# A two-block float32 model on one core: the depthwise convolution's accumulators and the engines of the norm behind it

## The chip, the cores and the metric

The kernel runs on one core of one Trainium2 chip. The metric is the device time of one execution in microseconds, lower is better. The core's engines run side by side: TensorE (PE; PEld is its weight load), VectorE (DVE), ScalarE (ACT), GpSimd (POOL) and SyncE (SP, which issues most transfers). SBUF is the working memory; PSUM, eight banks of 128x512 float32, holds matmul results and can be read and written by VectorE and ScalarE as well.

## The reference

A sequence of 512 tokens of width 1024 goes through two blocks. The first has two layers. Layer A mixes with a convolution, layer B with a sparse attention; the second block has an attention branch, a gated scan and a routed expert layer. Only layer A's mixer matters here:

```python
def conformer_conv(u, conv_w, conv_b, g, b):
    a, gl = jnp.split(u, 2, axis=-1)
    h = a * jax.nn.sigmoid(gl)
    h = jnp.pad(h, ((0, 0), (CONV_KERNEL - 1, 0), (0, 0)))
    h = lax.conv_general_dilated(h, conv_w[:, None, :], (1,), 'VALID',
                                 feature_group_count=CONV_WIDTH, ...) + conv_b
    return jax.nn.silu(layer_norm(h, g, b))
```

It is a depthwise convolution of 1536 channels with 31 taps along the sequence, followed by a layer norm over the channels and a SiLU. In the layer, `u`, a memory query and a gate come from one projection of `x`; the mixer's output and a cross-attention over a small memory are concatenated, multiplied by `silu(gate)`, projected by `a_w_out`, and go through a residual layer norm.

## The kernel before, in words

Activations are transposed: channels in the partitions, the 512 tokens along the free dimension. So the 1536 convolution channels are 12 tiles, `h0` to `h11`, each 128x542 with 30 zeros ahead. A float32 product is made of three matmuls (`mm3`, L164 to L166): operand and weight are each split in a high part (`hi`, a cast on ScalarE, L158 or L184) and the low rest (`lo`, a subtraction on VectorE or GpSimd, L159 or L187). `Weights` loads, splits and keeps weights in pieces of 128x1024 when they are first used; its attribute `lo` says which engine subtracts.

`layer_a` (L537) issues the work in this order. L545: twelve pairs of projections, and out of each pair `h_j` on VectorE (L552). Then the memory's keys and values (`mem_kv`, tiles `mk`, `ak`, `mvT`, `av`), four memory attentions (`mem_attn`, with the maximum `mmx` on VectorE and the exponential `mp` on ScalarE), and sixteen gates (L568), whose products L576 and L579 and the low halves of `y12` to `y15` are GpSimd's; gate tiles go to a DRAM buffer `a_gates`. Between the gates lie the keys and values of layer B (`bk`, `bv`).

The convolution (L585 to L604) has a first column, `h2`, that ScalarE multiplies and GpSimd adds. The other eleven are VectorE's: for each group of columns in the table `CGR` (L49) it runs over the 31 taps, and in a tap over the group's columns. One tap is one instruction, L602: the column shifted by `t` times a weight per partition, plus the accumulator. The first two columns of a group accumulate in a PSUM bank of the list `cv` (banks 6 and 7); a third one accumulates in the SBUF tile of tag `cva` (L594). `CGR` has one group of three, (7, 8, 9), so the third column is `h9`.

`st.add` squares each finished column on ScalarE and adds it up on GpSimd. `st.finish` sums over the channels with small matmuls (tile `cst`, L290), and spreads the mean and the reciprocal deviation over the partitions into PSUM (`Mb`, `Rb`). Then VectorE subtracts `Mb` from the twelve tiles (L607). L609 copies `Rb` to SBUF as `Rs`, since GpSimd works on SBUF. In the loop of L610 each tile is multiplied by the deviation (L614 on VectorE for every third tile, L616 on GpSimd for the others), scaled (L618), goes through the SiLU (L620 and L621) and the gate that was read back (L623), and is split for the next product; the low half is VectorE's for even tiles and GpSimd's for odd ones.

`out_proj` (L470) multiplies by `a_w_out`: for four output tiles the first eight of the 16 input tiles (`y12` to `y15`, `y0` to `y3`), then the other eight, then the remaining four output tiles in two halves of the tokens.

The program is written in a framework that keeps dependences by semaphores and chooses the order of each engine's instructions itself; each engine then works through its own list in that order, and waits where an operand isn't there. So an edit of a few lines can move the instructions of the whole layer.

Of the kernel before, what the change touches and what calls it, by code (L numbers as in the profile page):

```python
# [17 lines left out]
OP = mybir.AluOpType  # L18
# [27 lines left out]
NLO = 3  # L46
JMEM = 4
MLO = 6
CGR = (0, 1), (3, 4), (5, 6), (7, 8, 9), (10, 11)  # L49
NWARM = 8  # L50
WCUT = {0: 2, 2: 8}
WONE = 5
# [6 lines left out]
class Body:  # L59
# [249 lines left out]
    def run(self):  # L309
        nc = self.nc  # L310
# [8 lines left out]
        self.right = ExitStack()  # L319
        self.bk = self.right_pool("bk")  # L320
        if True:
            with self.phase("A", cva=1, slot=12, pcv=4, scr=2, asc=2, app=2, sq=2, accq=1, accs=1, back=4):
                with self.tc.tile_pool(name="mem", bufs=1) as self.mem:
                    self.layer_a()
            if self.stop == "a":
                self.right.close()
                return
            self.banks(mm=(0, 1), s=(2, 5), pt=(3, 4), o=(6, 7))
            with self.phase("B", slot=14, scr=4, asc=2, app=2, logit=3, alibi=2):
                self.layer_b()  # L330
# [206 lines left out]
    def layer_a(self):  # L537
        nc = self.nc
# [21 lines left out]
        Y = {}  # L560
        for h in range(4):
            f = self.scr("qm", tag="back")
            nc.scalar.copy(f, self.proj(W, 24 + h, self.X))
            o = self.mem_attn(self.split(f, f"qm{h}", lo="g"), kv, h)
            f = self.scr("mo")
# [19 lines left out]
        for j in (2,):  # L585
            for t in range(CK):
# [4 lines left out]
                    nc.gpsimd.tensor_tensor(p if t < CK - 1 else cs[j], acc, p, op=OP.add)  # L591
                acc = p
        for js in CGR:
            accs = [self.scr("cacc", tag="cva") if u == 2 else self.bank("cv", "cacc") for u in range(len(js))]  # L594
            for t in range(CK):
                for j, a in zip(js, accs):
                    wc = self.vec("conv_w", j * CK + t)
                    src = hs[j][:, t:t + T]
                    if t == 0:
                        nc.vector.tensor_scalar(a, src, wc, self.vec("conv_b", j), op0=OP.mult, op1=OP.add)  # L600
                    else:
                        nc.vector.scalar_tensor_tensor(a if t < CK - 1 else cs[j], src, wc, a, op0=OP.mult, op1=OP.add)  # L602
            for j in (2, *js) if 5 in js else js:
                st.add(cs[j])  # L604
        Rb, Mb = st.finish(CONVW, 1e-5)
        for c in cs:
            nc.vector.tensor_tensor(c, c, Mb, op=OP.subtract)  # L607
        Rs = self.scr("Rs", tag="accs")
        nc.scalar.copy(Rs, Rb)  # L609
        for j in range(12):  # L610
            c = cs[j]
            n = self.scr("cn", tag=("asc", "app")[j % 2])
            if j % 3 == 0:
                nc.vector.tensor_tensor(n, c, Rb, op=OP.mult)  # L614
            else:
                nc.gpsimd.tensor_tensor(n, c, Rs, op=OP.mult)  # L616
            c = n
            nc.scalar.activation(c, c, AF.Identity, bias=self.vec("a_ln_b", j), scale=self.vec("a_ln_g", j))  # L618
            th = self.scr("th")
            nc.scalar.activation(th, c, AF.Tanh, scale=0.5)  # L620
            nc.vector.scalar_tensor_tensor(c, th, 1.0, c, op0=OP.add, op1=OP.mult)  # L621
            y = self.back("gb", gd[j])
            nc.vector.scalar_tensor_tensor(y, c, 0.25, y, op0=OP.mult, op1=OP.mult)  # L623
            Y[4 + j] = self.split(y, f"y{j}", hi="s", lo="vg"[j % 2], x=2 <= j < 10, tag="slot" if j < 2 else "pcv")
        self.new_x()
        self.banks(alias=dict(Rb="cv", Mb="cv"), mm=(0, 1, 2, 5), pt=(3, 4), cv=(6, 7))

# [862 lines left out]
```

## Time and profile before

| | us |
|---|---|
| median of 3 runs | 2709.32 |
| lowest, highest | 2707.19, 2710.68 |
| the profiled execution | 2716.38 |
| its span, first to last instruction | 2714.4 |
| busy in it: PE, DVE, ACT, POOL | 2621.4, 2077.2, 1247.2, 952.8 |

The profile is of one execution. Busy time counts an engine's instructions from start to end, overlaps once; instructions of one engine overlap by some 0.08 us, so the distance between the starts of two of them is a little less than their duration. Matmuls are pipelined, so a busy TensorE need not be one at its peak. [...] An idle time is put down to the instruction whose completion ended it.

### The profile page before, as it was taken

The numbers are of one execution on the slowest core, as the hardware profiler recorded it, in microseconds if no ns is written. First come the engines' busy times: TensorE is split into PE (matmuls) and PEld (weight loads), VectorE is DVE, ScalarE is ACT, GpSimd is POOL, SyncE is SP. The second block draws the span as 40 slices with busy tenths as digits, with TensorE's granted clock in tenths as the row PEclk, the third lists the DMA queues.
The fourth block names the chain that finished last, engine by engine and source line by source line (L and its number), as shares of the span: only waits on it lengthen the run. The fifth ranks groups of instructions, "written<-read, shape, count | busy, mean of one in ns | idle before, by whom it ended". The sixth has DMA issues, their size and how long they took to land.

```text
span 2714.4 us, 40123 instructions
## 1 busy us (share of the span) xinstructions
PE 2621.4 (97%) x14581; PEld 2284.0 (84%) x14581; DVE 2077.2 (77%) x3926; ACT 1247.2 (46%) x2173; POOL 952.8 (35%) x654
## 2 busy tenths in 40 slices
PE   9989989999999999999999999999999999999998
PEld 7777879788889977788899999898898888888876
DVE  8999876695557678763679999888877877787765
ACT  4535554455545444333443555555543443343333
POOL 5965654332206555553431123223311121111201
PEclk9999999999999999999999999999999999999999
DMA  5233355223246311225733788788899899999952
GB/s 183 86 109 116 125 163 172 87 82 98 82 152 209 109 55 55 66 87 167 217 96 115 239 291 309 289 324 294 316 369 340 304 330 332 335 327 338 338 191 93
DMA packets 211958, 542.20 MB, mean 200 GB/s; under 512 B 18224, under 2 KB 105904, under 8 KB 192304
## 3 DMA queue, kind: packets, MB, share of 16 engines
q1 hardware_dynamic: 183488, 395.30, 44.3%
q0 software_dynamic: 18432, 134.23, 13.3%
q10 hardware_dynamic: 9840, 10.12, 1.2%
q8 instruction: 114, 1.87, 0.3%
q14 instruction: 84, 0.69, 0.1%
HBM read 468.99 MB, written 70.58 MB: 199 GB/s over the span
## 4 chain that ended last, share of the span: by engine, by line
PE 50%; DMA 14%; DVE 12%; issue 4%; ACT 2%; POOL 1%; SPq 0%; DVEq 0%; POOLq 0%; ACTq 0%
DMA grow<-peer_uv,pidx 9%; PE mm L164 9%; PE mm L165 9%; PE mm L166 8%; PE po L166 4%; PE po L164 4%; PE po L165 4%; DMA as<-a_spill 3%; PE out L164 2%; PE out L165 2%; PE out L166 2%; DVE pacc L1199 1%; DVE wlo L159 1%; DVE og L1312 1%; DVE hK L917 1%
## 5 line engine op out<-in xcount | busy, mean ns | idle before, releaser
L1189 POOL DMA_INDIRECT grow<-peer_uv,pidx x128 | 236.8, 1850 | 914.8 <-DVE pacc L1199 751.8
L158 ACT CAST whi<-wraw 128x1024 fp32r<-128x1024 f32 x360 | 377.6, 1050 | 383.9 <-PE mm L165 194.4
L159 POOL TENSOR_TENSOR wlo<-wraw,whi 128x1024 fp32r<-128x1024 f32 x157 | 380.7, 2427 | 419.6 <-ACT whi L158 360.9
L164 PE MATMUL po<-vhi,wh 128*128 128x512 f32 x768 | 297.1, 392 | 4.0 <-ACT wh L1351 4.0
L165 PE MATMUL po<-vlo,wh 128*128 128x512 f32 x768 | 299.0, 391 | 0.0
L159 DVE TENSOR_TENSOR wlo<-wraw,whi 128x1024 fp32r<-128x1024 f32 x203 | 260.1, 1283 | 48.2 <-ACT whi L158 45.4
L166 PE MATMUL po<-vhi,wl 128*128 128x512 f32 x768 | 273.6, 393 | 3.2 <-DVE wl L1352 3.2
L602 DVE SCALAR_TENSOR_TENSOR cacc<-h,vecs,cacc 128x512 f32<-128x512 f32 x319 | 240.0, 815 | 0.4
L1192 DVE SCALAR_TENSOR_TENSOR grow<-grow,hrow 128x1024 f32<-128x1024 f32 x128 | 156.6, 1223 | 101.2 <-DMA grow<-peer_uv,pidx 101.2
L166 PEld LDWEIGHTS po<-vhi,wl 128*128 128x128 f32 x768 | 143.9, 188 | 36.7 <-DVE wl L1352 6.6
L164 PEld LDWEIGHTS po<-vhi,wh 128*128 128x128 f32 x768 | 144.0, 188 | 34.2 <-ACT wh L1351 4.6
L165 PEld LDWEIGHTS po<-vlo,wh 128*128 128x128 f32 x768 | 144.3, 188 | 27.9
L159 DVE TENSOR_TENSOR vlo<-vraw,vhi 128x1024 fp32r<-128x1024 f32 x128 | 156.4, 1222 | 11.7 <-ACT vhi L158 11.6
L1199 DVE SCALAR_TENSOR_TENSOR pacc<-grow,pwc,pacc 128x1024 f32<-128x1024 f32 x127 | 162.8, 1282 | 2.3 <-ACT pwc L1195 1.8
L1194 ACT ACTIVATE pwc<-pac 128x1 f32<-128x1 f32 x128 | 25.9, 202 | 275.7 <-DVE grow L1192 275.6
L158 ACT CAST vhi<-vraw 128x1024 fp32r<-128x1024 f32 x128 | 133.8, 1046 | 34.4 <-DMA vraw<-peer_uv 18.1
L1351 ACT CAST wh<-as 128x384 fp32r<-128x384 f32 x103 | 52.6, 510 | 145.8 <-PE po L165 133.3
L1321 ACT COPY stage<-gp 128x512 f32<-128x512 f32 x96 | 96.9, 1101 | 44.9 <-PE gp L1319 44.9
L164 PE MATMUL mm<-X0h,whi 128*128 128x512 f32 (+2 forms) x294 | 109.8, 378 | 6.0 <-ACT pa L1181 2.6
L1319 PE MATMUL gp<-og,oh 128*128 128x128 bf16 x1152 | 95.7, 227 | 17.4 <-DVE og L1312 17.0
L165 PE MATMUL mm<-X2l,whi 128*128 128x512 f32 (+2 forms) x294 | 106.6, 363 | 0.6 <-DVE X2l L529 0.6
L164 PE MATMUL mm<-X2h,whi 128*128 128x512 f32 (+2 forms) x294 | 105.6, 359 | 1.4 <-ACT X2h L528 1.4
(984 smaller groups left out, 7762.8 us busy)
## 6 DMA issues: line engine op xcount, KB each, us to landing
wraw<-peer_uT SPq DMA_DIRECT2D x128, 512.0 KB, 5.7
vraw<-peer_uv SPq DMA_DIRECT2D x128, 512.0 KB, 7.0
gates<-stage SPq DMA_DIRECT2D x24, 1024.0 KB, 6.7
G<-gates SPq DMA_DIRECT2D x16, 1536.0 KB, 14.5
wraw<-a_w_in SPq DMA_DIRECT2D x43, 512.0 KB, 3.5
wraw<-c_w_in SPq DMA_DIRECT2D x42, 512.0 KB, 3.5
wraw<-b_w_in SPq DMA_DIRECT2D x39, 512.0 KB, 3.6
a_spill<-pa SPq DMA_DIRECT2D x103, 192.0 KB, 5.5
```

What stands on the lines that cost most here:

```text
L158: nc.scalar.copy(h, src)
L159: (nc.gpsimd if lo == "g" else nc.vector).tensor_tensor(l, src, h, op=OP.subtract)
L164: nc.tensor.matmul(ps, w[0], x[0], start=start, stop=False)
L165: nc.tensor.matmul(ps, w[0], x[1], start=False, stop=False)
L166: nc.tensor.matmul(ps, w[1], x[0], start=False, stop=stop)
L602: nc.vector.scalar_tensor_tensor(a if t < CK - 1 else cs[j], src, wc, a, op0=OP.mult, op1=OP.add)
L1189: nc.gpsimd.indirect_dma_start(out=gt, out_offset=None, in_=self.i["peer_uv"], in_offset=bass.IndirectOffsetOnAxis(ap=self.idx[:, n:n + 1] ...
L1192: nc.vector.scalar_tensor_tensor(gt[:, :D], gt[:, :D], 1.0, self.hrow, op0=OP.mult, op1=OP.mult, accum_out=ac)
L1199: nc.vector.scalar_tensor_tensor(self.acc, gt[:, D:], wc, self.acc, op0=OP.mult, op1=OP.add)
L1319: nc.tensor.matmul(gp[:, u * 128:(u + 1) * 128], oh2[:, bu[0], :, bu[1]], o[:, bu[0], :, bu[1]], start=n == 0, stop=n == 2)
L1321: nc.scalar.copy(stage[:, :, h + q:h + q + 4].rearrange("p n t -> p t n"), gp.rearrange("p (t n) -> p t n", t=4))
L1351: nc.scalar.copy(wh, a)
```

## The change

The group of three columns is gone: the eleven columns of VectorE are six groups of at most two, all in PSUM banks, the last with one column. The norm's multiplications by the deviation are all VectorE's and read `Rb` in PSUM; the copy `Rs` is gone. The low halves of the odd tiles are VectorE's as well.

```diff
-CGR = (0, 1), (3, 4), (5, 6), (7, 8, 9), (10, 11)
+CGR = (0, 1), (3, 4), (5, 6), (7, 8), (9, 10), (11,)
...
-            with self.phase("A", cva=1, slot=12, pcv=4, scr=2, asc=2, app=2, sq=2, accq=1, accs=1, back=4):
+            with self.phase("A", slot=12, pcv=4, scr=2, asc=2, app=2, sq=2, accq=1, accs=1, back=4):
...
         for js in CGR:
-            accs = [self.scr("cacc", tag="cva") if u == 2 else self.bank("cv", "cacc") for u in range(len(js))]
+            accs = [self.bank("cv", "cacc") for _ in js]
...
         for c in cs:
             nc.vector.tensor_tensor(c, c, Mb, op=OP.subtract)
-        Rs = self.scr("Rs", tag="accs")
-        nc.scalar.copy(Rs, Rb)
         for j in range(12):
             c = cs[j]
             n = self.scr("cn", tag=("asc", "app")[j % 2])
-            if j % 3 == 0:
-                nc.vector.tensor_tensor(n, c, Rb, op=OP.mult)
-            else:
-                nc.gpsimd.tensor_tensor(n, c, Rs, op=OP.mult)
+            nc.vector.tensor_tensor(n, c, Rb, op=OP.mult)
             c = n
...
-            Y[4 + j] = self.split(y, f"y{j}", hi="s", lo="vg"[j % 2], x=2 <= j < 10, tag="slot" if j < 2 else "pcv")
+            Y[4 + j] = self.split(y, f"y{j}", hi="s", lo="v", x=2 <= j < 10, tag="slot" if j < 2 else "pcv")
```

The order of the instructions moves at three places. The changed program's line numbers behind the edit are smaller by 3 or 5: its L611 is L614 before, its L616 and L618 are L621 and L623 before.

The first is VectorE in the middle of the convolution, around the last `h` tile, `h11`; `cacc_3000` is the SBUF accumulator of column 9, `cacc_2922` and `cacc_2923` are the PSUM banks of columns 5 and 6. Before:

```order
L602 SCALAR_TENSOR_TENSOR cacc_2923<-h6_721,vecs_70,cacc_2923 128x512
L602 SCALAR_TENSOR_TENSOR cacc_3000<-h9_922,vecs_70,cacc_3000 128x512
L602 SCALAR_TENSOR_TENSOR cacc_2922<-h5_654,vecs_70,cacc_2922 128x512
L552 SCALAR_TENSOR_TENSOR h11_1056<-th_1054,mm_992 128x512
L602 SCALAR_TENSOR_TENSOR cacc_2923<-h6_721,vecs_70,cacc_2923 128x512
L602 SCALAR_TENSOR_TENSOR cacc_3000<-h9_922,vecs_70,cacc_3000 128x512
L602 SCALAR_TENSOR_TENSOR cacc_2922<-h5_654,vecs_70,cacc_2922 128x512
```

Now:

```order
L602 SCALAR_TENSOR_TENSOR cacc_2923<-h6_721,vecs_70,cacc_2923 128x512
L602 SCALAR_TENSOR_TENSOR cacc_2922<-h5_654,vecs_70,cacc_2922 128x512
L602 SCALAR_TENSOR_TENSOR cacc_2923<-h6_721,vecs_70,cacc_2923 128x512
L552 SCALAR_TENSOR_TENSOR h11_1056<-th_1054,mm_992 128x512
L602 SCALAR_TENSOR_TENSOR cacc_2922<-h5_654,vecs_70,cacc_2922 128x512
L602 SCALAR_TENSOR_TENSOR cacc_2923<-h6_721,vecs_70,cacc_2923 128x512
L602 SCALAR_TENSOR_TENSOR cacc_2922<-h5_654,vecs_70,cacc_2922 128x512
```

Column 9 needed no bank, so its taps stood among those of two earlier groups; now two columns take turns and column 9 comes later, in a bank.

The second is VectorE in the norm, from the last subtraction of the mean on (`wlo` is a weight subtraction for `a_w_out`, `y0l` the first low half). Before:

```order
L607 TENSOR_TENSOR h_1056<-h_1056,Mb 128x512
L614 TENSOR_TENSOR cn<-h_219,Rb 128x512
L614 TENSOR_TENSOR cn<-h_414,Rb 128x512
L159 TENSOR_TENSOR wlo<-wraw,whi 128x1024 x2
L223 TENSOR_TENSOR bv_2558<-mvt,bv_2558 128x256
L621 SCALAR_TENSOR_TENSOR cn<-th,cn 128x512 x2
L159 TENSOR_TENSOR wlo<-wraw,whi 128x1024
L621 SCALAR_TENSOR_TENSOR cn<-th,cn 128x512 x2
L159 TENSOR_TENSOR wlo<-wraw,whi 128x1024
L623 SCALAR_TENSOR_TENSOR gb<-cn,gb 128x512
L187 TENSOR_TENSOR y0l<-gb,y0h 128x512
```

Now:

```order
L607 TENSOR_TENSOR h_1056<-h_1056,Mb 128x512
L611 TENSOR_TENSOR cn<-h_219,Rb 128x512
L611 TENSOR_TENSOR cn<-h_280,Rb 128x512
L611 TENSOR_TENSOR cn<-h_347,Rb 128x512
L611 TENSOR_TENSOR cn<-h_414,Rb 128x512
L223 TENSOR_TENSOR bv_2558<-mvt,bv_2558 128x256
L159 TENSOR_TENSOR wlo<-wraw,whi 128x1024
L616 SCALAR_TENSOR_TENSOR cn<-th,cn 128x512
L159 TENSOR_TENSOR wlo<-wraw,whi 128x1024
L616 SCALAR_TENSOR_TENSOR cn<-th,cn 128x512 x2
L159 TENSOR_TENSOR wlo<-wraw,whi 128x1024
L616 SCALAR_TENSOR_TENSOR cn<-th,cn 128x512
```

The multiplications of the tiles that GpSimd had stand on VectorE, two more of them right at the start.

The third is GpSimd behind the statistics. Before:

```order
L616 TENSOR_TENSOR cn<-h_280,Rs 128x512
L616 TENSOR_TENSOR cn<-h_347,Rs 128x512
L576 TENSOR_TENSOR g<-th,g 128x512
L579 TENSOR_TENSOR g<-g,ob 128x512
L187 TENSOR_TENSOR y14l<-g,y14h 128x512
L576 TENSOR_TENSOR g<-th,g 128x512
L579 TENSOR_TENSOR g<-g,ob 128x512
L576 TENSOR_TENSOR g<-th,g 128x512
L187 TENSOR_TENSOR y15l<-g,y15h 128x512
L616 TENSOR_TENSOR cn<-h_481,Rs 128x512
L616 TENSOR_TENSOR cn<-h_654,Rs 128x512
L187 TENSOR_TENSOR y1l<-gb,y1h 128x512
```

Now:

```order
L239 TENSOR_TENSOR rs_o<-rs_u,rs_r 128x4
L576 TENSOR_TENSOR g<-th,g 128x512
L579 TENSOR_TENSOR g<-g,ob 128x512
L187 TENSOR_TENSOR y14l<-g,y14h 128x512
L576 TENSOR_TENSOR g<-th,g 128x512
L579 TENSOR_TENSOR g<-g,ob 128x512
L576 TENSOR_TENSOR g<-th,g 128x512
L187 TENSOR_TENSOR y15l<-g,y15h 128x512
L270 TENSOR_TENSOR accs<-ar_3646,ar_3652 128x512
```

GpSimd keeps the seven operations of the last gates, and next has the sums of the layer's second norm.

## Rows read from the trace of the kernel before

**Rows 1.** The page: the span, and busy time of each engine.
```profile
span 2714.4 us, 40123 instructions
...
PE 2621.4 (97%) x14581; PEld 2284.0 (84%) x14581; DVE 2077.2 (77%) x3926; ACT 1247.2 (46%) x2173; POOL 952.8 (35%) x654
```

**Rows 2.** Stages of layer A: stretch, length, busy time per engine, clock, DMA.
```profile
core 0: us, PE busy (x) PEld busy (x) DVE busy (x) ACT busy (x) POOL busy (x), PEclk, DMA share, GB/s
131.50:222.50 91.00, 79.19 (x431) 68.75 (x430) 91.00 (x105) 30.88 (x53) 54.54 (x26) 0.94 0.33 99
222.50:320.00 97.50, 92.25 (x514) 79.32 (x512) 97.32 (x149) 62.42 (x127) 73.89 (x44) 1.00 0.43 139
320.00:331.20 11.20, 11.20 (x60) 11.20 (x61) 1.30 (x4) 2.56 (x5) 4.83 (x9) 0.58 0.33 114
331.20:372.10 40.90, 40.84 (x187) 33.26 (x185) 35.01 (x39) 26.61 (x43) 22.07 (x16) 1.00 0.40 122
380.30:452.30 72.00, 71.99 (x504) 67.67 (x504) 45.26 (x56) 31.99 (x48) 32.22 (x29) 0.97 0.65 205
```

**Rows 3.** Groups, DVE, 131.5 to 222.5: xcount | busy us, mean ns | idle before.
```profile
L602 DVE SCALAR_TENSOR_TENSOR cacc<-h,vecs,cacc 128x512 f32<-128x512 f32 x86 | 80.9, 1005 | 0.0
L602 DVE SCALAR_TENSOR_TENSOR h<-h,vecs,cacc 128x512 f32<-128x512 f32 x3 | 4.3, 1436 | 0.0
```

**Rows 4.** Groups, DVE, 222.5 to 320.6.
```profile
L602 DVE SCALAR_TENSOR_TENSOR cacc<-h,vecs,cacc 128x512 f32<-128x512 f32 x106 | 72.9, 744 | 0.1
```

**Rows 5.** Time line, DVE, 145.2 to 157.5: start us, us, what.
```profile
144.63 13.00 DVE L602 SCALAR_TENSOR_TENSOR cacc<-h,vecs,cacc 128x512 f32<-128x512 f32 x12
```

**Rows 6.** Time line, POOL, 145.2 to 164: start us, us, what [idle before <-releaser].
```profile
145.95 2.39 POOL L159 TENSOR_TENSOR wlo<-wraw,whi 128x1024 fp32r<-128x1024 f32 x1 [1.79 <-ACT whi L158]
148.95 2.41 POOL L159 TENSOR_TENSOR wlo<-wraw,whi 128x1024 fp32r<-128x1024 f32 x1 [0.61 <-ACT whi L158]
...
163.13 2.38 POOL L159 TENSOR_TENSOR wlo<-wraw,whi 128x1024 fp32r<-128x1024 f32 x1 [6.04 <-ACT whi L158]
```

**Rows 7.** Time line, DVE, 158.9 to 160.7.
```profile
158.82 2.06 DVE L602 SCALAR_TENSOR_TENSOR cacc<-h,vecs,cacc 128x512 f32<-128x512 f32 x3
```

**Rows 8.** Waits of PE, 125 to 382: us in total, times, longest.
```profile
PE mm L164 <- ACT mk L414: 5.2, 1, 5.2
PE msc L164 <- ACT mp L446: 5.1, 2, 3.5
...
PE cst L290 <- DVE h L602: 3.6, 1, 3.6
...
PE mvt L423 <- ACT mvT L420: 2.0, 1, 2.0
```

**Rows 9.** Time line, ACT, 198 to 212.
```profile
210.66 0.47 ACT L446 ACTIVATE mp<-msc,mmx 128x256 f32<-128x256 f32 x1 [11.26 <-DVE mmx L442]
```

**Rows 10.** Time line, DVE, 319 to 381.
```profile
318.41 0.76 DVE L602 SCALAR_TENSOR_TENSOR cacc<-h,vecs,cacc 128x512 f32<-128x512 f32 x1
319.20 0.75 DVE L602 SCALAR_TENSOR_TENSOR h<-h,vecs,cacc 128x512 f32<-128x512 f32 x1
...
331.26 1.29 DVE L607 TENSOR_TENSOR h<-h,Mb 128x512 f32<-128x512 f32 x2 [2.88 <-PE Mb L838]
...
379.05 2.35 DVE L159 TENSOR_TENSOR wlo<-wraw,whi 128x1024 fp32r<-128x1024 f32 x2
```

**Rows 11.** Time line, PE, around 323, 380 and 430.
```profile
323.01 3.55 PE L290 MATMUL cst<-ones,sq 128*128 128x1 f32 x16
...
380.31 0.80 PE L166 MATMUL out<-y4h,wlo 128*128 128x512 f32 x1 [3.05 <-DVE wlo L159]
...
430.00 1.03 PE L290 MATMUL lnst<-ones,sq 128*128 128x1 f32 x8
```

**Rows 12.** Groups, DVE, the norm, 331.2 to 388.6.
```profile
L621 DVE SCALAR_TENSOR_TENSOR cn<-th,cn 128x512 f32<-128x512 f32 x12 | 15.0, 1275 | 1.6 <-ACT th L620 1.6
L623 DVE SCALAR_TENSOR_TENSOR gb<-cn,gb 128x512 f32<-128x512 f32 x12 | 12.6, 1064 | 3.3 <-DMA gb<-a_gates 3.2
...
L607 DVE TENSOR_TENSOR h<-h,Mb 128x512 f32<-128x512 f32 x12 | 7.3, 682 | 2.9 <-PE Mb L838 2.9
```

**Rows 13.** Groups, DVE, beside the last gates, 341.9 to 355.6.
```profile
L621 DVE SCALAR_TENSOR_TENSOR cn<-th,cn 128x512 f32<-128x512 f32 x4 | 5.2, 1326 | 1.6 <-ACT th L620 1.6
```

**Rows 14.** Groups, POOL, the norm, 331.2 to 390.6.
```profile
L616 POOL TENSOR_TENSOR cn<-h,Rs 128x512 f32<-128x512 f32 x8 | 10.3, 1291 | 14.4 <-DVE gb L623 6.5 <-issue 4.4 <-ACT Rs L609 3.5
```

## The prediction

> **What bounds the kernel now.** The page's busy shares come first: TensorE is busy for 97% of the span and VectorE for 77% [rows 1]. A mean over six stages says little about a change inside one of them, so the next view is the table by stage [rows 2]. It covers layer A, the only part that the edit touches. From 131.5 to 222.5 us VectorE is busy for all of 91.0 us and TensorE for 79.19, at a granted clock of 0.94; from 222.5 to 320.0 both are nearly full; from 320 to 331.2 VectorE has 1.30 us of work and TensorE's clock is down to 0.58. So the convolution runs at VectorE's pace, and TensorE waits in its first half.
>
> Why is VectorE slow there? In the groups by line, 86 taps of L602 took 80.9 us between 131.5 and 222.5, and three last taps 4.3 us [rows 3]; later 106 taps took 72.9 us, 0.69 us each [rows 4]. The time line shows the pattern: twelve taps in 13.00 us [rows 5], where 12 x 0.69 = 8.3, while GpSimd starts a 2.4 us weight subtraction about every 3 us [rows 6]. While GpSimd idles before 163.13, three taps take 2.06 us [rows 7]. What is special in this stretch is column 9, whose accumulator lies in SBUF: its tap reads two SBUF tiles. The PSUM columns' taps do not stretch: the 106 of rows 4 average 744 ns, beside 73.89 us of GpSimd work [rows 2, 4].
>
> TensorE's waits tell who is kept: 5.2, 5.1 and 2.0 us on ScalarE copies before the statistics, then 3.6 us on the last tap itself [rows 8]. Those copies are late because of VectorE: one softmax exponential sat 11.26 us waiting for a maximum that stood in VectorE's queue behind the taps [rows 9].
>
> **The change part by part.** The sum is made against the profiled execution, 2716.4 us with its launch, 0.3% above the median of 2709.3; I subtract the gain from the median.
>
> *(a) Up to the statistics.* All eleven columns now accumulate in PSUM, so no tap reads two SBUF tiles. VectorE's 89 taps of rows 3 took 80.9 + 4.3 = 85.2 us; at 0.69 they take 61.4, which frees 23.8 us. Against it, column 11 is alone in its group: back-to-back taps into one accumulator start 0.79 us apart (318.41 and 319.20 [rows 10]) in place of 0.66. The order puts seven more of such pairs at the end, 7 x 0.13 = 0.9, call it 1 us. Two banks for eleven columns cost nothing else, since VectorE runs one tap at a time anyway. VectorE is then done at 320.0 - 23.8 + 1 = 297.2. TensorE must get there too: it stood at 320.0 - 3.6 = 316.4. If the 12.3 us of earlier waits go, and the clock of 0.94 over 91 us with them (5.5 us), it stands at 298.6. I keep 3 of the 12.3 us, since a softmax has a latency of its own: 301.6. Gain 320.0 - 301.6 = 18.4 us. The bounds are 21.4 (no wait kept, 298.6) and 3.6 (every earlier wait and the low clock stay, only the wait on the last tap goes).
>
> [...] In rows 7 one tap in three belongs to column 9, and with GpSimd idle the SBUF and the PSUM accumulator both cost 0.66 us a tap, so moving it to PSUM adds nothing. [...]
>
> *(b) Statistics.* From the last tap to the first subtraction of the mean, 319.95 to 331.26 [rows 10], 11.3 us pass. The 32 column sums start on a TensorE that has just stood still: 16 of them take 3.55 us at 323.01, 0.21 each; eight like them take 1.03 us at 430.00, about 0.11 each at the full clock [rows 11]. If TensorE comes there without a pause, 32 x 0.10 = 3.2 us go; I take 3. Bounds: 0, and 4.4 with the few matmuls behind them at the low clock (0.58 in that stretch [rows 2]).
>
> *(c) The norm.* What TensorE waits for next is the first weight subtraction of the second half of a_w_out's rows: it starts at 379.05 on VectorE, 47.8 us after 331.26 [rows 10], and TensorE goes on at 380.31 after 3.05 us of waiting [rows 11]. Before it VectorE's order has 40 operations of 128x512, four weight subtractions and one small one. At 0.6 us (twelve L607 in 7.3 [rows 12]) and 1.2 us (two in 2.35 [rows 10]) that is 24 + 4.8 + 0.3 = 29.1 us. The waits before L621 and L623 are 1.6 + 3.3 = 4.9 us [rows 12]; the remaining 13.8 us is stretch: L621 and L623 average 1275 and 1064 ns where L607 has 682 [rows 12], both reading two SBUF tiles while GpSimd does its multiplications (eight L616, 1291 ns each [rows 14]) and low halves. The change puts 48 operations and three weight subtractions ahead of the same point: 28.8 + 3.6 + 0.3 = 32.7 us, 3.6 more. The waits are kept, 4.9. Of the stretch, what GpSimd's remaining seven gate operations cause stays: beside them, from 341.9 to 355.6, four L621 took 1326 ns each [rows 13], 4 x 0.64 = 2.6 us, and with the subtractions and the product beside them I take 4. So 32.7 + 4.9 + 4 = 41.6 in place of 47.8: gain 6.2 us. TensorE has 40.84 us of its own work from 331.2 to 372.1 [rows 2]; with 1.2 us for the subtraction, VectorE's 42.8 is last by 2, so the most that (c) can give is 49.1 - 40.9 = 8.2. The least is -3.6: all the stretch stays and the added work lies on top. The removed copy Rs (one ScalarE operation) was ahead of GpSimd's multiplications only and gives nothing more. Behind 380.31 the six new low halves come in time as before: VectorE has 45.26 us of work in the next 72.0, TensorE 71.99 [rows 2], so nothing is gained or lost there; the orders of the layers after A are the same.
>
> Sum: 18.4 + 3 + 6.2 = 27.6 us, so 2709.3 - 27.6 = 2681.7, about **2682 us**. All bounds at once give 2709.3 - 34 = 2675 and 2709.3 - 0 = 2709.
>
> **The rivals.** *TensorE's waits are latency, not lateness.* The waits on copies and softmax stay and only the last tap's wait goes: 3.6 + 3 + 6.2 = 12.8 us, 2696.5. For it: from 222.5 on TensorE is busy for 92.25 of 97.5 us though VectorE is just as full, so both may be near their limits. Against it: the 11.26 us of rows 9.
>
> *The norm becomes the bound, slower.* VectorE gets 14 more operations (eight multiplications, six low halves), 14 x 0.6 = 8.4 us by the last low half. If the stretch of 13.8 us comes from the gates and not from GpSimd's norm, and TensorE still reaches the sums at 316 or later, VectorE is late by all of it: 2709.3 + 8.4 = 2717.7. It decides once less than 8.4 us of stretch goes. Against it: only 2.6 to 4 us of stretch lies beside the gates [rows 13].
>
> *It does not do what it says.* A PSUM tap still reads its source column from SBUF; if that alone collides with GpSimd, the taps stretch as before: 2709. Rows 4 speak against it.
>
> **How the numbers follow.** A measurement of this kernel tells 0.2%, 5.4 us, from no change. The forecast, with its own range of 2674 to 2690, has 0.74; the latency rival, 2690 to 2703, has 0.18; no change 0.04; slower 0.04. The range from 2674 to 2698 takes in the bounds of (b) and (c) and the centre of the first rival, and leaves out about 2 in 10. Faster has 0.92, the same 0.04, slower 0.04.
>
> **What would show it.** In the changed profile: no tap of L602 over 0.8 us; the last tap near 297 to 302 us; TensorE's waits on ScalarE between 131 and 222 us down from 12.3 to some 3; column sums at 0.11 us; GpSimd without norm rows after its gates; VectorE's L621 and L623 near 680 ns but for the first few; the second half of the output projection starting near 353 in place of 380.3, and everything behind it moved by the same amount. Taps that still stretch, TensorE waits that stay at 12 us, or a norm over 48 us long would make it wrong.

## The result and the profile after

The changed kernel takes **2679.53 us** (median of 4 runs, 2676.43 to 2685.79), the kernel before 2710.0 (2707.19 to 2713.88). The ratio is 0.9889, 95% interval 0.9868 to 0.9911: 30 us faster, between 24 and 36. The prediction was 2682 us, in a range from 2674 to 2698.

The page of the changed kernel, its span and its engines, beside [rows 1]:

```profile
span 2674.7 us, 40111 instructions
...
PE 2609.2 (98%) x14581; PEld 2277.3 (85%) x14581; DVE 2058.3 (77%) x3940; ACT 1246.3 (47%) x2172; POOL 935.5 (35%) x640
```

The profiled execution took 2676.43 us, the one before 2716.38. That is 40.0 us, 10 more than the medians differ. Both profiles agree about where the change acts: the output projection of layer A ends at 452.3 us before and at 421.1 now, 31.2 us earlier. The other 8.5 us by which the spans differ lie behind that point, where but for a few neighbours that changed places the instructions are in the same order; the medians don't show them.

The table by stage, cut where the stages of the changed kernel end (columns as in [rows 2]; PEclk is the clock granted to TensorE, as a share of its full clock):

```profile
core 0: us, PE busy (x) PEld busy (x) DVE busy (x) ACT busy (x) POOL busy (x), PEclk, DMA share, GB/s
131.50:222.50 91.00, 91.00 (x517) 79.72 (x516) 89.89 (x143) 46.40 (x87) 67.55 (x37) 1.00 0.39 121
222.50:299.30 76.80, 76.11 (x441) 66.63 (x439) 74.03 (x109) 47.03 (x91) 56.76 (x32) 1.00 0.45 151
299.30:310.60 11.30, 11.27 (x61) 10.76 (x62) 2.56 (x6) 3.80 (x7) 4.84 (x9) 0.70 0.26 86
310.60:350.10 39.50, 38.87 (x173) 31.26 (x171) 34.69 (x52) 28.34 (x44) 10.84 (x7) 1.00 0.41 134
350.10:421.10 71.00, 70.45 (x504) 66.28 (x505) 50.99 (x64) 36.85 (x56) 30.83 (x27) 1.00 0.68 214
```

In the first stage TensorE was busy for 79.19 of 91 us at a clock of 0.94 [rows 2]; now it is busy for all of 91 at the full clock, and VectorE did 143 instructions there in place of 105. The groups of VectorE in that stage say why, beside [rows 3] with their means of 1005 and 1436 ns:

```profile
L602 DVE SCALAR_TENSOR_TENSOR cacc<-h,vecs,cacc 128x512 f32<-128x512 f32 x112 | 75.9, 749 | 0.0
...
L602 DVE SCALAR_TENSOR_TENSOR h<-h,vecs,cacc 128x512 f32<-128x512 f32 x3 | 2.2, 737 | 0.0
```

No tap is stretched any more, although GpSimd works for 67.55 us beside them, more than the 54.54 before. The 12.3 us of waits of [rows 8] are gone; between 125 and 382 us TensorE waits for this much:

```profile
PE out L164 <- ACT whi L158: 1.1, 2, 0.9
PE cst L290 <- DVE h L602: 0.7, 1, 0.7
```

VectorE's time line gives the marks of [rows 10]: last tap, first subtraction of the mean, first weight subtraction of the output projection's second half:

```profile
298.53 0.75 DVE L602 SCALAR_TENSOR_TENSOR h<-h,vecs,cacc 128x512 f32<-128x512 f32 x1
...
310.59 7.27 DVE L607 TENSOR_TENSOR h<-h,Mb 128x512 f32<-128x512 f32 x12 [1.38 <-PE Mb L833]
...
350.17 2.36 DVE L159 TENSOR_TENSOR wlo<-wraw,whi 128x1024 fp32r<-128x1024 f32 x2
```

So the last tap ends at 299.28 (before 319.95), the statistics take 11.3 us (11.3), and from the mean to the weight subtraction pass 39.6 us (47.8). In the norm (VectorE's groups from 310.5 to 366; L616 and L618 are L621 and L623 of [rows 12], with 1275 and 1064 ns) most of the stretch is gone too:

```profile
L616 DVE SCALAR_TENSOR_TENSOR cn<-th,cn 128x512 f32<-128x512 f32 x12 | 9.5, 802 | 1.1 <-ACT th L615 1.1
...
L618 DVE SCALAR_TENSOR_TENSOR gb<-cn,gb 128x512 f32<-128x512 f32 x12 | 8.1, 691 | 5.7 <-DMA gb<-a_gates 5.5
```

GpSimd has nothing of the norm there (its groups of the same stretch), where it had the eight multiplications of [rows 14]:

```profile
L576 POOL TENSOR_TENSOR g<-th,g 128x512 f32<-128x512 f32 x3 | 4.3, 1446 | 11.4 <-ACT th L575 11.4
L579 POOL TENSOR_TENSOR g<-g,ob 128x512 f32<-128x512 f32 x2 | 3.5, 1727 | 0.2
L187 POOL TENSOR_TENSOR y14l<-g,y14h 128x512 fp32r<-128x512 f32 x1 | 1.8, 1836 | 2.5 <-ACT y14h L184 2.5
L187 POOL TENSOR_TENSOR y15l<-g,y15h 128x512 fp32r<-128x512 f32 x1 | 1.3, 1294 | 0.0
```

What the prediction did not have is the columns one by one: along VectorE's order each of the trace's 330 taps and 11 first products goes to its column. Mean duration of a column's 31 instructions, in us (the longest of the changed kernel is a first product; its longest tap took 0.77):

```
run                               SBUF column   its mean   longest   all other columns
before                            9             1.559      2.94      0.743 to 0.752
changed kernel                    none                     0.82      0.745 to 0.760
norm alone (below)                9             1.423      2.89      0.746 to 0.755
column 6 in SBUF (below)          6             1.478      2.87      0.746 to 0.758
before, GpSimd spared (below)     9             1.089      2.85      0.744 to 0.751
```

In the kernel before, the whole stretch lay on column 9: 30 taps x (1.56 - 0.75) = 24 us, against the 23.8 that the prediction freed. It is uneven: 19 of the column's 30 taps took over 0.85 us, each beside an instruction of GpSimd, and the others 0.74.

### The profile page after: what moved, and what is told of

Same layout as the page of the kernel before. It is cut to its first block, busy times and chain, and to the rows that moved or that the text cites. A ratio compares the mean times of both kernels' runs of the same rounds, so it can differ in the third digit from the quotient of the medians.

```text
span 2674.7 us, 40111 instructions
## 1 busy us (share of the span) xinstructions
PE 2609.2 (98%) x14581; PEld 2277.3 (85%) x14581; DVE 2058.3 (77%) x3940; ACT 1246.3 (47%) x2172; POOL 935.5 (35%) x640
## 4 chain that ended last, share of the span: by engine, by line
PE 58%; DVE 10%; DMA 10%; issue 3%; ACT 2%; POOL 1%; SPq 0%; DVEq 0%; POOLq 0%; ACTq 0%
PE mm L164 9%; PE mm L165 9%; PE mm L166 9%; DMA grow<-peer_uv,pidx 8%; PE po L166 6%; PE po L165 6%; PE po L164 6%; PE out L164 2%; PE out L165 2%; PE out L166 2%; DVE wlo L159 1%; PE gp L1314 1%; DMA as<-a_spill 1%; DVE pacc L1194 1%; DVE og L1307 1%
## 5 line engine op out<-in xcount | busy, mean ns | idle before, releaser
L602 DVE SCALAR_TENSOR_TENSOR cacc<-h,vecs,cacc 128x512 f32<-128x512 f32 x319 | 218.0, 749 | 0.6
L165 PE MATMUL mm<-X0l,whi 128*128 128x512 f32 (+2 forms) x294 | 106.3, 362 | 0.7 <-DVE X0l L529 0.7
```

The lines of the kernel that those rows point to most:

```text
L165: nc.tensor.matmul(ps, w[0], x[1], start=False, stop=False)
```

## The experiments

In these runs, too, each kernel stands beside the kernel before on the same chip; that one's median was between 2702.8 and 2711.6. "Mean to end" is the time from the first subtraction of the mean to the end of layer A's output projection (121.1 us before, 110.6 in the changed kernel).

**1. The groups alone.** The kernel before with

```diff
-CGR = (0, 1), (3, 4), (5, 6), (7, 8, 9), (10, 11)
+CGR = (0, 1), (3, 4), (5, 6), (7, 8), (9, 10), (11,)
...
-            accs = [self.scr("cacc", tag="cva") if u == 2 else self.bank("cv", "cacc") for u in range(len(js))]
+            accs = [self.bank("cv", "cacc") for _ in js]
```

> The kernel before with the new groups alone: eleven columns in six groups, all accumulators in PSUM; the norm with its multiplications and low halves on GpSimd stays. Theory (the accumulator's place frees VectorE, and that carries most of the gain): every L602 tap at 0.75 us, the last tap at 299 us as in the changed kernel (299.28), the norm as long as before (47.8 us from the first subtraction of the mean to the second half's first weight subtraction); time 2710 - 20.7 = 2689 us, between 2686 and 2693. Rival (the norm carries most): the last tap still comes 20 us earlier, but TensorE gives part of it back in the norm, whose GpSimd operations now collide with more work; time above 2696.

Measured: 2693.42 us (2690.48 to 2695.54), ratio 0.9923 (0.9893 to 0.9953), so 21 us faster. The last tap ends at 300.0, the mean to end is 120.1 us. That is the theory, with the time just over the upper end of its range: the gain up to the last tap passes through the norm undiminished, and the norm itself is as long as before. TensorE's waits from 125 to 395 us show what bounds the norm then, above all the weight subtraction for which it waited before, too [rows 11]:

```profile
PE out L166 <- DVE wlo L159: 3.9, 1, 3.9
```

**2. The norm alone.** The changed kernel with the old table, and `h9` in SBUF again.

```diff
-CGR = (0, 1), (3, 4), (5, 6), (7, 8), (9, 10), (11,)
+CGR = (0, 1), (3, 4), (5, 6), (7, 8, 9), (10, 11)
...
-            accs = [self.bank("cv", "cacc") for _ in js]
+            accs = [self.scr("cacc", tag="cva") if u == 2 else self.bank("cv", "cacc") for u in range(len(js))]
```

> The changed kernel with the old groups: the group of three columns with its accumulator in SBUF is back, the norm stays on VectorE. Theory (the parts add up): the last tap at 320 us as in the kernel before, column 9's taps near 1.56 us; the gain is the norm's alone, 7 to 10 us, time 2700 to 2703. Rival (the two parts help each other: the norm only gains because the conv was early and TensorE full): a gain of under 4 us, time over 2706.

Measured: 2703.24 us (2696.07 to 2712.13), ratio 0.9967 (0.9950 to 0.9984), 9 us faster. The last tap came at 315.3, not at 320: column 9's taps happened to be a little shorter (1.42 in place of 1.56 us, 4.2 us in all). The mean to end is 114.1 us, 7.0 less than before. The two parts add up within their intervals: 0.77% and 0.33% make 1.10%; the change has 1.11%, and 0.97% when it was run again (run 10).

**3. The accumulator's place by itself.** The changed kernel, six groups, with column 6 in SBUF:

```diff
...
-            accs = [self.bank("cv", "cacc") for _ in js]
+            accs = [self.scr("cacc", tag="cva") if j == 6 else self.bank("cv", "cacc") for j in js]
```

> The changed kernel with its six groups, but the accumulator of column 6 alone in SBUF. No group has three columns, so this is the accumulator's place by itself. Theory (two SBUF inputs beside GpSimd's work make a tap slow): column 6's 30 taps, which run from 129 to 176 us in the changed kernel, take about 1.5 us each in place of 0.75, all others stay at 0.75; 22 to 24 us more on VectorE, the last tap near 318 to 322, time 2698 to 2702. Rival (the group of three columns and its order cost the time before): column 6's taps at 0.75, time 2680.

Measured: 2708.64 us (2700.66 to 2717.29), ratio 0.9987 (0.9967 to 1.0007). VectorE's groups from 100 to 195 us look as they did before the change:

```profile
L602 DVE SCALAR_TENSOR_TENSOR cacc<-h,vecs,cacc 128x512 f32<-128x512 f32 x91 | 84.1, 990 | 0.0
```

The taps of column 6 average 1.478 us, all others 0.75; the last tap ends at 319.3, the output projection 24.8 us later than in the changed kernel. So the place of one accumulator of eleven gives back nearly all of the gain, without a group of three. By the ratios the run is 0.98% slower than the changed kernel, 27 us, and 24.8 of them show in the profile up to the end of the output projection. The time is 6 us over the upper end of what was expected; no run shows where these came from.

**4. Three banks.** The other way round: the group of three stays, its third accumulator goes to a third bank.

```diff
...
-        self.banks(alias=dict(st="cv", Rb="cv", Mb="cv"), mm=(0, 1), pt=(3, 4), s=(2,), o=(5,), cv=(6, 7))
+        self.banks(alias=dict(st="cv", Rb="cv", Mb="cv", o="s"), mm=(0, 1), pt=(3, 4), s=(2,), cv=(5, 6, 7))
...
-            accs = [self.scr("cacc", tag="cva") if u == 2 else self.bank("cv", "cacc") for u in range(len(js))]
+            accs = [self.bank("cv", "cacc") for _ in js]
```

> The kernel before with its group of three columns, but the third accumulator in a third PSUM bank (bank 5, which the memory attention's output gives up: it shares bank 2 with the scores). The norm stays as before. Theory (the accumulator's place decides, not the grouping): every tap at 0.75 us, the last tap near 299, time as with the new groups alone, 2686 to 2693, plus at most 6 us if the shared bank makes TensorE wait. Rival (the grouping decides): taps of the group of three stay long, time 2705 to 2712.

Measured: 2710.73 us (2705.33 to 2726.42), ratio 1.0012 (0.9987 to 1.0036): nothing gained. On the taps the theory holds: all eleven columns average 0.75 us, and the last tap ends at 287.0, 33 us earlier than before and 12 earlier than in the changed kernel. Yet the output projection begins at 349.7 us (before 349.5). With scores and output of the memory attention in one bank the framework, which plans the order, put the last of the four attentions behind the taps, and TensorE waits for its softmax (waits from 125 to 382 us):

```profile
PE msc L164 <- ACT mp L446: 10.6, 2, 7.1
...
PE mpT L454 <- ACT mp L450: 2.7, 1, 2.7
```

The stage from the last tap to the output projection shows it at a clock of 0.80 with VectorE mostly idle:

```profile
287.00:349.70 62.70, 54.03 (x302) 49.73 (x303) 26.39 (x43) 29.53 (x59) 18.64 (x18) 0.80 0.26 84
```

A faster VectorE was worth here what TensorE could use of it. The 6 us that were allowed for the shared bank were far too few.

**5 and 6. The norm's two halves.** Each is the changed kernel with one of GpSimd's two tasks given back.

```diff
-            Y[4 + j] = self.split(y, f"y{j}", hi="s", lo="v", x=2 <= j < 10, tag="slot" if j < 2 else "pcv")
+            Y[4 + j] = self.split(y, f"y{j}", hi="s", lo="vg"[j % 2], x=2 <= j < 10, tag="slot" if j < 2 else "pcv")
```

> The changed kernel, but the low halves of the odd tiles are GpSimd's again; all multiplications by the deviation stay on VectorE. Read from the first subtraction of the mean to the end of the output projection: 121.1 us before, 110.6 in the changed kernel. Theory (the stretch of 13.8 us comes from all that GpSimd does in the norm, in proportion to its time: eight multiplications of 1.3 us, six low halves): about half of the norm's gain is lost, 114 to 117 us, time 2683 to 2686. Rival (the multiplications alone did it): 110 to 112 us, time as the changed kernel, 2680.

```diff
+        Rs = self.scr("Rs", tag="accs")
+        nc.scalar.copy(Rs, Rb)
...
-            nc.vector.tensor_tensor(n, c, Rb, op=OP.mult)
+            if j % 3 == 0:
+                nc.vector.tensor_tensor(n, c, Rb, op=OP.mult)
+            else:
+                nc.gpsimd.tensor_tensor(n, c, Rs, op=OP.mult)
```

> The changed kernel, but two of three multiplications by the deviation are GpSimd's again, from the copy Rs; all low halves stay on VectorE. Theory (in proportion): 115 to 118 us from the first subtraction of the mean to the end of the output projection, time 2684 to 2688. Rival (the multiplications alone did it): all of the norm's gain is lost, 119 to 121 us, time 2688 to 2691.

Measured: with the multiplications alone on VectorE (5) 2680.87 us (2677.85 to 2682.66), ratio 0.9892 (0.9862 to 0.9921), mean to end 110.3 us; with the low halves alone (6) 2695.07 us (2686.58 to 2699.86), ratio 0.9937 (0.9912 to 0.9961), mean to end 116.6 us. With both on GpSimd it was 120.1 (run 1). The average of the 24 instructions L616 and L618 (L621 and L623) goes along: 0.746 us in the changed kernel, 0.759 in run 5, 0.892 in run 6, 1.028 in run 1. In the medians the two runs differ by 14 us, more than the 6 of the profiles, with intervals that overlap a little. So in these profiles it was not in proportion: once the multiplications are VectorE's, the low halves on GpSimd cost nothing; as long as GpSimd multiplies, they cost 3.5 us. Run 5 comes out as its rival said (110 to 112 us). Run 6 comes out as its theory said (115 to 118) and not its rival (119 to 121), but its time lies above both, and no run shows why. Of the 6 us to the end of the projection, a part is the clock: TensorE waits 1.6 and 0.9 us for its operands in the projection, and the granted clock is 0.51 from 354.8 to 361.7 us, where it stays at 1.00 in the changed kernel.

**7, 8, 9. The clock in the statistics.** The prediction had given this stage 3 us and it gave nothing. TensorE's time line of the changed kernel shows the column sums, beside [rows 11]:

```profile
299.33 0.38 PE L290 MATMUL cst<-ones,h 128*128 128x1 f32 x2 [0.73 <-DVE h L602]
...
300.92 3.30 PE L290 MATMUL cst<-ones,sq 128*128 128x1 f32 x16
```

Fourteen sums take 1.6 us, 0.11 each, and the next sixteen 3.3, 0.21 each (two of the 32 sums ran long before, at 279 us). The stage cut where the clock changes:

```profile
299.30:301.20 1.90, 1.87 (x17) 1.87 (x17) 0.31 (x1) 1.89 (x4) 0.25 (x1) 1.00 0.56 168
301.20:304.30 3.10, 3.10 (x16) 3.10 (x16) 0.47 (x2) 0.22 (x1) 2.10 (x1) 0.50 0.07 21
304.30:308.00 3.70, 3.70 (x16) 3.51 (x16) 0.55 (x3) 1.46 (x3) 2.49 (x8) 0.50 0.38 140
308.00:310.60 2.60, 2.60 (x16) 2.29 (x16) 1.22 (x2) 0.23 (x1) 0.00 (x0) 0.99 0.09 28
```

The clock is at half (0.50) from 301.2 to 308, while TensorE has no idle time. Was it the sums or the pause of 0.73 us ahead of them? Run 7 made the sums wider (the changed kernel, in `Stats`):

```diff
-nc.tensor.matmul(ps[:, c0 + u:c0 + u + 1], src[:, tt * 128:(tt + 1) * 128], b.ones[:, 0:1],
+nc.tensor.matmul(ps[:, (c0 + u) * 64:(c0 + u) * 64 + 64], src[:, tt * 128:(tt + 1) * 128], b.ones[:, 0:64],
...
```

> The changed kernel with one thing more: every sum over channels is done against 64 columns of ones in place of one (64 equal sums, of which one is read). In the changed kernel the sums at 299.3 us begin at 0.11 us each and at 300.9 the granted clock falls to half although TensorE is never idle; it is back at 308. Theory (it is the one-column sums that lose the clock, not the pause of 0.7 us ahead of them): the clock stays at 1.00 from 299 to 311, the 32 sums take 3.5 us in place of 4.9, the first subtraction of the mean comes 9 us after the last tap in place of 11.3, the end of the output projection 3 us earlier: time 2676 to 2678. Rival (the pause loses it, or something before the sums): the clock falls at the same place, the wider sums take 0.21 us each, time 2680 or up to 2 more.

Measured: 2676.91 us (2675.48 to 2686.25), ratio 0.9887 (0.9863 to 0.9912), not to be told from the changed kernel. The clock was 0.95 from 300.9 to 304.3 and 0.50 from 304.3 to 308.0, with the first sum at 301.66; the sums took 4.6 us. The theory is refuted: with 64 columns the clock fell all the same, 2.3 us after the first sum. The rival's 0.21 us a sum did not come either: the first fourteen wide sums took 0.11 us each, as the narrow ones. Run 8 was to take the pause away:

```diff
+            if j == 9:
+                fill = self.bank("pt", "fill")
+                for _ in range(8):
+                    nc.tensor.matmul(fill, self.X[0][0][:, :128], self.X[0][0], start=True, stop=True)
```

> The changed kernel with eight needless products of 128x512 (1.9 us) among the gates, so that TensorE reaches the channel sums later than VectorE's last tap and has no pause of 0.7 us ahead of them. Theory (the pause costs the clock): the clock stays at 1.00 through the 32 sums, they take 3.5 us, and the end of the output projection comes 1 to 2 us earlier counted from the last tap. Rival (the sums themselves cost it, pause or not): the clock falls to half 1.5 to 3 us after the first sum, the sums take 4.7 to 5.4 us, and everything behind is later by the pause's rest, 1.2 us.

It didn't: the framework ordered the products otherwise, a pause of 0.66 us stood ahead of the sums (first at 299.56), and the clock was 0.75 from 301 to 303 and 0.50 behind. One run, 2697.88 us; nothing follows. Run 9 took the pause away from the other side, by an earlier last tap:

```diff
-MLO = 6
+MLO = 8
```

> The changed kernel, but the two weight subtractions of layer B's keys and values that VectorE has between its last taps (286.7 and 290.7 us, 4.2 us together) go to GpSimd. VectorE's last tap comes about 4 us earlier, near 295, and TensorE, which reaches the channel sums near 296.5 in its new order, should have no pause ahead of them. Theory (the pause of 0.7 us costs the clock): the clock stays at 1.00 through the sums, which take 3.5 us. Rival (the sums themselves cost it): no pause, and the clock falls to half 1.5 to 3 us after the first sum all the same. For the time: TensorE is full up to the end of the output projection, so at most the pause and the low clock can be gained, 0 to 4 us, 2676 to 2681.

Measured: the last tap ends at 294.9, TensorE has no wait before the sums, and the 30 sums that stand there all run at the full clock, 3.4 us in all:

```profile
296.45 0.28 PE L290 MATMUL cst<-ones,h 128*128 128x1 f32 x2
...
297.93 1.93 PE L290 MATMUL cst<-ones,sq 128*128 128x1 f32 x16
```

Its clock, cut in the same way:

```profile
296.40:299.70 3.30, 3.30 (x32) 3.30 (x32) 0.00 (x0) 0.00 (x0) 3.30 (x2) 1.00 0.47 160
...
301.00:304.40 3.40, 3.40 (x18) 3.40 (x18) 0.00 (x0) 0.78 (x2) 3.36 (x3) 0.51 0.47 152
304.40:305.50 1.10, 1.10 (x11) 1.10 (x11) 0.67 (x2) 0.28 (x1) 0.77 (x5) 1.00 0.10 30
```

The fall comes at 301.0, behind the sums, and lasts 3.4 us in place of 6.8. From the first sum to the first subtraction of the mean pass 8.4 us in place of 11.3. But to the end of the output projection it is 122.4 us, against 121.8 in the changed kernel: the nine products of a gate that TensorE has there ahead of the mean stand behind it here. Of the time nothing can be seen: 2681.67 us (2678.13 to 2685.09), ratio 0.9926 (0.9906 to 0.9945), where the changed kernel had 0.9889 and, in the next run, 0.9903. Run 3 settles what run 9 left open. There, too, TensorE comes to the sums without a wait (it is busy for all of the 5.8 us ahead of them), and the clock falls among the sums:

```profile
320.40 0.28 PE L290 MATMUL cst<-ones,h 128*128 128x1 f32 x2
...
321.88 2.45 PE L290 MATMUL cst<-ones,sq 128*128 128x1 f32 x16
```

```profile
320.40:323.10 2.70, 2.70 (x27) 2.70 (x26) 0.00 (x0) 1.32 (x2) 2.70 (x2) 1.00 0.70 202
323.10:329.90 6.80, 6.80 (x34) 6.80 (x34) 1.02 (x3) 0.75 (x2) 3.35 (x9) 0.50 0.54 186
```

So the pause is not needed. Without one the clock fell in both profiles, 2.7 (run 3) and 4.5 us (run 9) after the first sum. Behind a pause of 0.66 to 0.76 us it fell in all seven (the changed kernel twice, runs 1, 5, 6, 7 and 8), 1.2 to 3.1 us after it. What it falls for stays open: the sums stand ahead of the fall every time, but 64 columns in place of one did not prevent it, and no run here leaves the sums out.

**10. The changed kernel again**, in the same hour as runs 5 to 7.

> The changed kernel unaltered, on the same chip and in the same hour as the three others, to compare them with: 2680 us, ratio 0.989, last tap near 299.3, output projection done near 421.

Measured: 2685.44 us (2677.68 to 2697.53), ratio 0.9903 (0.9879 to 0.9927). Last tap 303.6, output projection done at 427.6: 4.3 and 6.5 us later than in the first profile, 3.0 of it before the first tap. From the first tap to the last it is 277.2 us, against 275.9 in the first profile and 295.8 in the kernel before, so 18.5 to 19.8 us is the fairer figure for the gain in the taps.

**11. The tap by itself.** A program of VectorE's tap in stages of 48 (two accumulators in turn) or 24 (one), with GpSimd idle or subtracting beside it.

```diff
+STAGES = ("ss", 0, 0), ("pp", 0, 0), ("ss", 1024, 0), ("pp", 1024, 0), ("ps", 1024, 0), ("s", 512, 1), ("s", 0, 1), ("p", 0, 1)
...
+                    nc.gpsimd.tensor_tensor(lo[:, :size], raw[:, :size], hi[:, :size], op=OP.subtract)
...
+                    nc.vector.scalar_tensor_tensor(t, src[:, 1 + n % 30:1 + n % 30 + T], w, t, op0=OP.mult, op1=OP.add)
```

> The model is left out whole; what runs is the tap alone, in stages of 48 (two accumulators in turn) or 24 (one): accumulators in SBUF or PSUM, GpSimd idle or subtracting 128x1024 tiles (14) or 128x512 tiles (28) beside it. Theory (a tap with two SBUF inputs waits for GpSimd's instruction): with GpSimd idle SBUF and PSUM accumulators both near 0.66 us from start to start with two in turn; with GpSimd subtracting, PSUM taps stay at 0.66 and SBUF taps come at well over 1 us; in the stage with one of each, the SBUF tap alone is slow. Also read: one PSUM accumulator in every tap 0.79 us, one SBUF accumulator the same. [...]

The groups on the page of the profile (the letter is the accumulator's place, the number the stage; stages 2 to 4 run beside 14 subtractions of 128x1024 on GpSimd, which end before the taps do in stages 2 and 4, so that the means of acc2s and acc4s mix stretched taps and others):

```profile
L343 DVE SCALAR_TENSOR_TENSOR acc2s<-src,vecs,acc2s 128x512 f32<-128x512 f32 x48 | 61.2, 1348 | 0.0
...
L343 DVE SCALAR_TENSOR_TENSOR acc4s<-src,vecs,acc4s 128x512 f32<-128x512 f32 x24 | 38.2, 1590 | 0.0
L343 DVE SCALAR_TENSOR_TENSOR acc3p<-src,vecs,acc3p 128x512 f32<-128x512 f32 x48 | 31.9, 748 | 0.0
...
L343 DVE SCALAR_TENSOR_TENSOR acc4p<-src,vecs,acc4p 128x512 f32<-128x512 f32 x24 | 17.9, 744 | 0.0
```

Beside GpSimd an SBUF tap is slow and a PSUM tap is not, in the same stage with taps in turn (acc4s and acc4p). There VectorE's time line shows the pattern: while GpSimd subtracts, each SBUF tap lasts 2.17 us (the first 2.59), each PSUM tap 0.74:

```profile
184.39 0.74 DVE L343 SCALAR_TENSOR_TENSOR acc4p<-src,vecs,acc4p 128x512 f32<-128x512 f32 x1
185.04 2.17 DVE L343 SCALAR_TENSOR_TENSOR acc4s<-src,vecs,acc4s 128x512 f32<-128x512 f32 x1
187.14 0.74 DVE L343 SCALAR_TENSOR_TENSOR acc4p<-src,vecs,acc4p 128x512 f32<-128x512 f32 x1
```

GpSimd pays too: its 14 subtractions take 38.34 us beside SBUF taps and 32.30 beside PSUM taps (its time line, stages 2 and 3), 2.74 and 2.31 us each:

```profile
76.92 38.34 POOL L339 TENSOR_TENSOR lo<-raw,hi 128x1024 fp32r<-128x1024 f32 x14 [76.48 <-ACT hi L336]
141.77 32.30 POOL L339 TENSOR_TENSOR lo<-raw,hi 128x1024 fp32r<-128x1024 f32 x14 [26.52 <-ACT hi L336]
```

The SBUF tap from 185.04 to 187.21 us ends 0.55 us after the subtraction that had begun before it, at 183.88:

```profile
183.88 2.78 POOL L339 TENSOR_TENSOR lo<-raw,hi 128x1024 fp32r<-128x1024 f32 x1
```

The kernel before shows the same: each of the 19 taps of column 9 that took over 0.85 us ends 0.55 us after the end of an instruction of GpSimd that ran beside it. So does this one (VectorE's time line, 146.1 to 148), beside the subtraction of [rows 6] that ends at 148.34:

```profile
145.95 2.94 DVE L602 SCALAR_TENSOR_TENSOR cacc<-h,vecs,cacc 128x512 f32<-128x512 f32 x1
```

Why a tap with two SBUF inputs ends there, no run shows.

With GpSimd idle, the place makes no difference. VectorE's time line, 48 taps with two accumulators in turn, then 24 with one:

```profile
5.45 31.88 DVE L343 SCALAR_TENSOR_TENSOR acc0s<-src,vecs,acc0s 128x512 f32<-128x512 f32 x48
...
40.21 31.69 DVE L343 SCALAR_TENSOR_TENSOR acc1p<-src,vecs,acc1p 128x512 f32<-128x512 f32 x48
...
280.35 18.86 DVE L343 SCALAR_TENSOR_TENSOR acc6s<-src,vecs,acc6s 128x512 f32<-128x512 f32 x24
...
300.96 18.96 DVE L343 SCALAR_TENSOR_TENSOR acc7p<-src,vecs,acc7p 128x512 f32<-128x512 f32 x24
```

That is 0.66 us a tap in SBUF and in PSUM, and 0.79 a tap with a single accumulator in either. The equal cost that the prediction read off [rows 7] holds: the PSUM taps are 0.004 us shorter with two in turn, 0.004 longer with one.

**12. GpSimd spared.** The kernel before, column 9 in SBUF, but the weights' low parts in its stretch on VectorE:

```diff
-            W.lo = "v" if name == "b" and h >= MLO else "g"
+            W.lo = "v" if name == "a" else "g"
...
+            W.lo = "g" if j < 10 else "v"
...
```

> The kernel before with its SBUF accumulator, but from the eleventh pair of projections to the last memory query VectorE subtracts the weights' low parts and GpSimd is left with the memory queries, the eighth's sums and the column it adds up. A diagnosis and no cure: VectorE gets some 25 subtractions of 1.2 us, 30 us. Theory (GpSimd's subtractions stretch column 9's taps): the column's mean tap falls from 1.56 us to under 1.0 where GpSimd is idle; the time changes little, 2705 to 2725. Rival (the tap with two SBUF inputs is slow by itself in this stretch): 1.5 us a tap, time 2730 or more.

Measured: 2705.35 us in one run (the kernel before in its one run beside it 2703.83). GpSimd's busy time from 131.5 to 222.5 us fell from 54.54 to 34.88, the mean of column 9 from 1.559 to 1.089 us, and 10 taps were left that took over 0.85 us, where there had been 19, each beside something that GpSimd still did. It was a little over the 1.0 that was expected, with seven weight subtractions among what was left to GpSimd; the stretch follows GpSimd's work, not the tap.

## Why the prediction was right, and where its sizes were off

**What bounds the kernel.** Right. VectorE paced the convolution, and what stretched its taps was column 9 alone; runs 3, 11 and 12 show the cause from three sides: the place of the accumulator, the tap alone, and GpSimd's work beside it.

**(a) Up to the statistics, 18.4 us forecast, 20.7 measured** (0.9 of it an earlier start of the first tap; 18.5 to 19.8 from first to last tap). TensorE came to the sums at 298.6, the value that the prediction had worked out for no wait at all; that it fits to the tenth is luck, since the start was 0.9 us earlier. The term that was mis-sized is the 3 us kept for the softmax's latency: the 11.26 us of [rows 9] and the waits of [rows 8] were lateness, as none is left. VectorE ended at 299.28 where 297.2 was forecast. It now waits at times itself, which the prediction put at nothing: its busy time from 222.5 to 299.3 is 74.03 of 76.80 us, where it was 97.32 of 97.50. Most of these waits are for ScalarE (1.3 us within the softmax, 0.8 for a copy of `bk`), 0.2 us for a product of TensorE. So VectorE was last after all, by 0.7 us.

**(b) The statistics, 3 us forecast, 0 measured.** Two steps failed. The first is the condition, a TensorE that comes there without a pause and so keeps its clock: VectorE was last, 0.73 us of waiting stayed, and the clock fell 1.9 us into the sums. Without a pause it falls as well, as run 3 shows. The second is that the shorter sums were taken for a shorter way to the mean. The 30 sums (the prediction counted all 32) did get shorter, 4.9 us in place of 6.6. But the products that spread the mean, `Mb`, come 5.3 us behind the end of the sums where it had been 3.6. The first sum and `Mb` before, and `Mb` now:

```profile
320.00 0.59 PE L290 MATMUL cst<-ones,h 128*128 128x1 f32 x2 [3.57 <-DVE h L602]
...
330.17 1.05 PE L838 MATMUL Mb<-ident,st 128*128 128x128 f32 x8
```

```profile
309.50 1.06 PE L833 MATMUL Mb<-ident,st 128*128 128x128 f32 x8
```

TensorE is busy all that time: before with 16 products of the memory's 256 columns and 4 transposes, now with 11 and 2 and, in part at the half clock, nine products of 128x512 for a gate. So the 1.7 us that the sums gained went into work that no longer stands behind the mean. In run 9 the sums took 3.4 us and the mean came 2.9 us earlier, the size of the term, and the end of the output projection was no earlier for it: where TensorE is full, (b) does not add to (c).

**(c) The norm, 6.2 us forecast, 10.5 measured.** VectorE's way to the second half's weight subtraction took 39.6 us where 41.6 was forecast, a gain of 8.2. The work (48 operations and three weight subtractions) and the waits were as counted; what was mis-sized is the remaining stretch, taken at 4 us: VectorE's busy time from 310.6 to 350.1 is 34.69, which leaves 2.0 over the 32.7 of unstretched work. TensorE is busy for 38.87 of these 39.50 us and so bounds the norm now. The step that failed is that nothing is gained behind 380.31. From the weight subtraction to the end of the projection it took 73.3 us and takes 71.0. Before, TensorE had waited 2.2, 1.5 and 3.05 us just ahead of 380.31 (two weight casts, then [rows 11]), and its clock was down behind them (a row of the view of [rows 8], and the stretch behind 380.3):

```profile
PE out L164 <- ACT whi L158: 3.8, 2, 2.2
```

```profile
380.30:387.00 6.70, 6.69 (x22) 5.37 (x23) 6.67 (x7) 1.48 (x3) 1.29 (x1) 0.72 0.77 231
```

Now the waits there are 0.9 and 0.2 us, and the clock stays at 1.00 up to 421.10. The 10.5 us pass the limit of 8.2 that the prediction had set for (c), by this clock and by the three input tiles of a gate's projection that TensorE had done ahead of the mean. So (b) and (c) share one sum: 9.2 forecast, 10.5 measured.

The errors are of both signs, 18.4 + 3 + 6.2 against 20.7 + 0 + 10.5 = 31.2 in the profiles; the runs give 30. That the forecast came so near is in part luck: (b) gave nothing, and (a) and (c) gave more than was forecast.

**The rivals.** Latency in place of lateness: refuted by the missing waits. The norm as the bound, slower: refuted, though with a lesson in run 6, where two thirds of the multiplications on GpSimd cost 6 us up to the end of the projection, part of it by TensorE's clock. That PSUM taps stretch too: refuted by run 11, 0.748 us beside a working GpSimd.

## What to carry to other kernels

When the same instruction takes 0.75 us here and 1.5 there, sort its instances by operand before looking for a cause: here the mean of 1005 ns hid one column at 1.56 and all others at 0.75. On VectorE beside a working GpSimd, put one of the two operands of a long chain of accumulations in PSUM; it was as fast as SBUF when GpSimd idled, and when GpSimd worked a tap took 0.74 us in place of 2.17 (0.75 in place of 1.56 over a whole column here). And before a bank is taken for that from another stage, look who waits there: run 4 freed 33 us of VectorE's time and gained nothing.

## What was not expected of the hardware

TensorE's granted clock fell to half (0.50; 0.51 in run 9) while the engine was busy without a gap, among or just behind the sums over channels: 1.9 us after the first sum behind a pause of 0.73 us, for 6.8 us; 2.7 us after it without any pause (run 3), for 6.8 us; and 4.5 us after it in run 9, for 3.4 us. Sums of 64 columns in place of one did not prevent it. And GpSimd is slower for it, too: beside SBUF taps its subtraction of 128x1024 took 2.74 us, beside PSUM taps 2.31.
